# A list scheduler gets other matmul steps and a shared VectorE/GpSimd port

## The chip, the cores and the metric

The kernel runs on one core of a Trainium2 chip. The core has five engines that run their own instruction streams in order: TensorE (PE in the profile, with its weight loads as PEld), VectorE (DVE), ScalarE (ACT), GpSimd (POOL) and SyncE (SP, which here only issues DMAs). The metric is the device time of one launch in microseconds, as the median of several runs. Lower is better.

## What is computed

Two layers of a hybrid decoder on a sequence of 512 tokens with 1024 features, and a final RMS norm. Every layer has two branches that are merged by gates, an output projection and a feed-forward part:

```python
def hybrid_layer(x, c, positions, cos, sin, w_ada, b_ada, w_in, ...):
    mod = (c @ w_ada + b_ada)[:, None, :]
    sh_m, sc_m, g_m, sh_f, sc_f, g_f = jnp.split(mod, 6, axis=-1)
    h = rms_norm(x) * (1 + sc_m) + sh_m
    proj = h @ w_in
    x_lru, q_down, kv_down, k_rope, gate_a, gate_b = jnp.split(proj, IN_SPLIT_POINTS, axis=-1)
    y_a = rg_lru(causal_depthwise_conv(x_lru, conv_w, conv_b), positions, ...)
    y_b = mla(q_down, kv_down, k_rope, cos, sin, ...)
    y = jax.nn.sigmoid(gate_a) * y_a + jax.nn.sigmoid(gate_b) * y_b
    x = x + g_m * (y @ w_out)
    h = rms_norm(x) * (1 + sc_f) + sh_f
    gate, up = jnp.split(h @ w_ffn_in, 2, axis=-1)
    return x + g_f * ((jax.nn.silu(gate) * up) @ w_ffn_out)
```

`c` is one vector of 1024 numbers, so the modulation is a matrix by a vector. `rg_lru` is a recurrence over the tokens (a scan), `mla` an attention with 8 heads. All inputs are float32.

## The kernel before

Activations lie feature-major: a tile is [128 features, 512 tokens]. A product is made of three matmuls per 128x128 weight block, because both factors are split into a high and a low part in a reduced float32 type (`mm3`: high x high, high x low, low x high). Of a weight block that lands by DMA in `raw`, ScalarE makes the high part `whi` and VectorE the low part `wlo` (in the first products GpSimd makes `wlo` for the feature tiles 1 to 7). There are three buffers each of `raw`, `whi` and `wlo`, two of `graw` (the weights of the modulation), and eight PSUM banks.

The start is special. The first products (`first_products`) run by feature tile 0 to 7 into six accumulators at once, 17 matmuls per tile, each tile as soon as its scale and shift are known. Scale and shift come from columns of `w_ada` (`first_mods`): for some tiles TensorE multiplies them (`pt<-cols,wa`, plain float32, 64 columns), for the others VectorE sums them up (`wacc<-wa,cols,wacc`) and TensorE only adds over partitions (`pt<-ones,wacc`). The result lands in `mod0_0` and `mod0_1`, and ScalarE and VectorE then make the tiles `hh` and `hl` that the products take.

After that come, in layer 0 and again in layer 1: the recurrent branch (`x_lru`, `conv` with its three steps `xc`, `gates`, `decay`, `recur` with the scan `ri<-a,ri`), the attention (`make_qk`, `scores`, `transposes` with `pl<-pt,ph`, `values`), the gates, the merge, the output projection and the feed-forward products. In layer 0 VectorE also sums up the other modulation vectors in the background (`macc<-graw,cols,macc`).

What sets the order: the body does not issue instructions but records them. `order()` then plays a greedy schedule with assumed durations (`cost`), latencies and buffer counts. Whenever an engine is free in that play, it takes the ready call with the longest remaining path. The calls are issued in the order of the play, and each engine of the chip runs its own list strictly in that order, with the waits that the data needs. So a figure in `cost` decides only where an instruction stands.

There is one exception to "same calls". While TensorE is idle in the play and the first products are not through, `fill()` puts in a matmul on zeros, as many as fit the idle time, so that the clock of TensorE stays up:

```python
            if o is None or self.fill not in issued or self.fill_end in issued or now < FILL_FROM or fills[0] >= FILL_MAX:
                return
            fills[0] += 1
            busy["PE"] = True
            res.append(o)
            heapq.heappush(events, (now + clock(now, o.dur, True), next(seq), "free", "PE"))
```

A fill is 256 columns in bfloat16, and no result hangs on it; but whatever stands behind it on TensorE comes after it.

## Time and profile before

| what | value |
|---|---|
| median of 3 runs (lowest to highest) | 1367.15 us (1366.49 to 1367.56) |
| span of the profiled execution, first to last instruction | 1361.9 us |
| median less that span | 5.3 us |
| TensorE busy | 1339.6 us, 98% |
| VectorE / ScalarE / GpSimd busy | 872.4 / 623.5 / 213.2 us |
| mean granted TensorE clock | 0.995 |
| TensorE matmul records, of them fills | 6330, 57 |

The profile gives no other time of the profiled execution than its span, so the 5.3 us around it are taken from the median. In a row of the trace the first number is the start in us from the span's start and the second how long it took; "[... <-X]" is the idle time of the engine before it and what ended it. Every call goes through one helper line, so all rows read L503, and tiles have to be told by their names. The matmuls are pipelined: one of 512 columns reads 0.39 us long while the next starts 0.227 us after it, so the step from start to start counts, and the gaps that the trace calls idle are shorter than the time lost.

### The profile page before, as it was taken

How to read it: one execution, taken by the hardware profiler on the slowest of the kernel's cores; microseconds unless marked ns; L12 is line 12 of the kernel's file. 1: busy time of each engine (PE TensorE's matmuls, PEld its weight loads, DVE VectorE, ACT ScalarE, POOL GpSimd, SP SyncE). 2: the span in 40 equal slices, each digit the busy share in tenths (PEclk: the TensorE clock that was granted, in tenths of full speed). 3: DMA queues.
4: the chain of work that ended last, by engine and by line, in shares of the span. 5: the costliest groups of instructions: out<-in, count | busy, mean ns of one | idle time of the engine just before them, and what ended most of it. 6: DMA issues, size and time to landing. Idle time of an engine off the chain costs nothing.

```text
span 1361.9 us, 17108 instructions
## 1 busy us (share of the span) xinstructions
PE 1339.6 (98%) x6330; PEld 1117.8 (82%) x6330; DVE 872.4 (64%) x1478; ACT 623.5 (46%) x963; POOL 213.2 (16%) x238
## 2 busy tenths in 40 slices
PE   8999989999999999999999999999999999999997
PEld 7788878887888888888888888888888888888887
DVE  5898799788856455556869887667673333333344
ACT  5585856644432222322356767855452322232223
POOL 1613334413000000000040243413400000000000
PEclk9999989999999999999999999999999999999999
DMA  9636344334655556555635333311433323433232
GB/s 300 200 96 168 103 124 140 124 117 137 194 182 164 163 159 206 178 170 184 203 86 141 92 86 100 94 47 47 124 89 98 89 75 104 120 93 95 77 88 81
DMA packets 251297, 174.92 MB, mean 128 GB/s; under 512 B 12767, under 2 KB 235341, under 8 KB 251213
## 3 DMA queue, kind: packets, MB, share of 16 engines
q1 hardware_dynamic: 251212, 173.82, 42.3%
q8 instruction: 50, 0.82, 0.2%
q14 instruction: 35, 0.28, 0.1%
HBM read 167.50 MB, written 2.10 MB: 125 GB/s over the span
## 4 chain that ended last, share of the span: by engine, by line
PE 84%; DVE 6%; DMA 5%; issue 2%; POOL 1%; ACT 1%; SPq 1%; ACTq 0%; DVEq 0%; POOLq 0%
PE mm L503 75%; PE s L503 4%; PE o L503 3%; DMA graw<-in_w_ada_dram 2%; PE pt L503 2%; DMA wa<-in_w_ada_dram 2%; DMA raw<-in_w_in_dram 1%; DVE macc L503 1%; DVE ri L503 1%; DVE wlo L503 1%; DVE xc L503 1%; POOL w L503 1%; DVE wacc L503 1%; SPq L503 1%; DVE sc L503 0%
## 5 line engine op out<-in xcount | busy, mean ns | idle before, releaser
L503 ACT ACTIVATE whi<-raw 128x1024 fp32r<-128x1024 f32 (+2 forms) x226 | 219.7, 973 | 581.3 <-PE mm L503 371.1
L503 DVE TENSOR_TENSOR wlo<-raw,whi 128x1024 fp32r<-128x1024 f32 (+2 forms) x218 | 249.3, 1145 | 205.5 <-ACT whi L503 201.2
L503 PE MATMUL mm<-fh,wlo 128*128 128x512 f32 x672 | 261.9, 390 | 0.0
L503 PE MATMUL mm<-fh,whi 128*128 128x512 f32 x672 | 261.7, 389 | 0.0
L503 PE MATMUL mm<-fl,whi 128*128 128x512 f32 x672 | 261.6, 389 | 0.0
L503 PE MATMUL mm<-hh,whi 128*128 128x512 f32 x408 | 161.3, 396 | 0.0
L503 PE MATMUL mm<-hl,whi 128*128 128x512 f32 x408 | 160.2, 393 | 0.0
L503 PE MATMUL mm<-hh,wlo 128*128 128x512 f32 x400 | 156.3, 391 | 0.0
L503 PEld LDWEIGHTS mm<-fl,whi 128*128 128x128 f32 x672 | 126.1, 188 | 26.4 <-DVE fl L503 0.2
L503 PEld LDWEIGHTS mm<-fh,wlo 128*128 128x128 f32 x672 | 126.1, 188 | 26.4 <-DVE wlo L503 0.3
L503 PEld LDWEIGHTS mm<-fh,whi 128*128 128x128 f32 x672 | 126.2, 188 | 26.0
L503 PE MATMUL mm<-ah,whi 128*128 128x512 f32 (+1 forms) x363 | 139.7, 385 | 0.0
L503 PE MATMUL mm<-ah,wlo 128*128 128x512 f32 (+1 forms) x363 | 139.3, 384 | 0.0
L503 PE MATMUL mm<-al,whi 128*128 128x512 f32 (+1 forms) x363 | 139.0, 383 | 0.0
L503 DVE SCALAR_TENSOR_TENSOR macc<-graw,cols,macc 128x512 f32<-128x512 f32 x140 | 103.8, 777 | 24.1 <-DMA graw<-in_w_ada_dram 23.7
L503 DVE TENSOR_TENSOR sg<-sg,mm 128x512 f32<-128x512 f32 x42 | 28.9, 688 | 111.1 <-PE mm L503 111.1
L503 PEld LDWEIGHTS mm<-hl,whi 128*128 128x128 f32 x408 | 77.0, 189 | 15.5 <-DVE hl L503 0.5
L503 PEld LDWEIGHTS mm<-hh,whi 128*128 128x128 f32 x408 | 77.0, 189 | 15.1 <-DVE whi L503 0.2
L503 PEld LDWEIGHTS mm<-hh,wlo 128*128 128x128 f32 x400 | 75.4, 189 | 15.8 <-POOL wlo L503 0.3
L503 PEld LDWEIGHTS mm<-ah,wlo 128*128 128x128 f32 x363 | 68.2, 188 | 13.3
L503 PEld LDWEIGHTS mm<-al,whi 128*128 128x128 f32 x363 | 68.2, 188 | 13.1
L503 PEld LDWEIGHTS mm<-ah,whi 128*128 128x128 f32 x363 | 68.2, 188 | 13.1
(266 smaller groups left out, 2173.9 us busy)
## 6 DMA issues: line engine op xcount, KB each, us to landing
raw<-in_w_ffn_in_dram SPq DMA_DIRECT2D x88, 512.0 KB, 3.9
graw<-in_w_ada_dram SPq DMA_DIRECT2D x80, 512.0 KB, 4.8
raw<-in_w_in_dram SPq DMA_DIRECT2D x49, 512.0 KB, 4.0
raw<-in_w_ffn_out_dram SPq DMA_DIRECT2D x32, 384.0 KB, 3.5
raw<-in_w_ffn_out_dram SPq DMA_DIRECT2D x32, 320.0 KB, 3.2
wa<-in_w_ada_dram SPq DMA_DIRECT2D x32, 256.0 KB, 5.6
raw<-in_w_out_dram SPq DMA_DIRECT2D x16, 512.0 KB, 3.9
raw<-in_w_uq_dram SPq DMA_DIRECT2D x24, 128.0 KB, 3.5
```

Source lines behind the costliest of these rows:

```text
L503: o.call(*(real(v) for v in o.a), **{k: real(v) for k, v in o.k.items()})
```

## The change

Three things in the planner change. The assumed TensorE time of a float32 matmul that is not in the reduced type falls from at least 207 ns to at least 107 ns. That of a matmul in the reduced type (all the `mm3` products) rises: 512 columns from 213.5 to 223.8 ns, 128 columns from 53.4 to 106 ns; 3 ns are added to each as before. And a VectorE or GpSimd call of the kinds tensor_tensor and scalar_tensor_tensor with two wide inputs in SBUF is now `shared`: when the other engine runs such a call in the play, it waits for its end.

```diff
-                 "npred", "ready", "bytes", "live")
+                 "npred", "ready", "bytes", "live", "shared")
...
         op.dur = self.cost(op, eng, method, a, k, outs, ins)
+        op.shared = eng in ("DVE", "POOL") and method in ("tensor_tensor", "scalar_tensor_tensor") and 2 == sum(
+            isinstance(x, Ref) and x.root.tag not in BANKS and x.shape[-1] > 1 for x in ins
+        )
...
             op.live = n > 32
-            return max(207.0, n * 1.667) if lhs.dtype == F32 else max(53.0, n * 0.417)
+            if lhs.dtype == F32:
+                return max(107.0, n * 1.667)
+            return n * 0.417 if lhs.dtype == BF16 else max(106.0, n * 0.417 + 10.3)
...
+        shared = {"DVE": 0.0, "POOL": 0.0}
...
                     d = clock(now, d, o.live)
+                if o.shared:
+                    other = "POOL" if e == "DVE" else "DVE"
+                    d += max(0.0, shared[other] - now)
+                    shared[e] = now + d
```

The rest of the diff deletes comments, which moves the helper line from L503 to L513. The calls are the same ones, except that TensorE gets 198 fills in place of 57 (141 more matmuls) and ScalarE 58 table loads in place of 51. The lists of all engines differ by shifts over a few places.

The first place is TensorE's list in the first products, at feature tile 5 (`hh_42`, `hl_50`, `whi_132`, `wlo_133`); `pt_120` is the scale and shift of the tiles 6 and 7. Before:

```order
247 L503 MATMUL mm_57_365<-hl_49_587,whi_118_595 128x512
248 L503 MATMUL mm_57_365<-hh_41_556,wlo_119_607 128x512
249 L503 MATMUL o_58_369<-hh_41_556,whi_118_595 128x512
250 L503 MATMUL o_58_369<-hl_49_587,whi_118_595 128x512
251 L503 MATMUL pt_120_657<-ones_83,wacc_125_539 128x64 x2
252 L503 MATMUL mm_53_345<-hh_42_565,whi_132_611 128x512
253 L503 MATMUL mm_53_345<-hl_50_628,whi_132_611 128x512
254 L503 MATMUL mm_53_345<-hh_42_565,wlo_133_630 128x512
255 L503 MATMUL pt_120_657<-ones_83,wacc_130_544 128x64 x2
```

Now, where the pair of rows 464 and 465 is the last of 41 fills that stand there one behind the other:

```order
464 L513 LDWEIGHTS fill_w_77
465 L513 MATMUL fill_4_87<-fill_x_75,fill_w_77 128x256
466 L513 MATMUL mm_53_384<-hl_50_756,whi_132_639 128x512
467 L513 MATMUL mm_53_384<-hh_42_646,wlo_133_668 128x512
468 L513 MATMUL mm_54_389<-hl_50_756,whi_132_639 128x512
469 L513 MATMUL mm_54_389<-hh_42_646,wlo_133_668 128x512
470 L513 MATMUL s_55_391<-hl_50_756,whi_132_639 128x512
471 L513 MATMUL s_55_391<-hh_42_646,wlo_133_668 128x512
472 L513 MATMUL s_56_396<-hl_50_756,whi_132_639 128x512
473 L513 MATMUL pt_120_786<-ones_83,wacc_125_594 128x64 x2
474 L513 MATMUL s_56_396<-hh_42_646,wlo_133_668 128x512
475 L513 MATMUL mm_57_402<-hl_50_756,whi_132_639 128x512
```

The six `hh` x `whi` matmuls of tile 5 have gone ahead of the fills, and the scale and shift of the tiles 6 and 7 (`pt_120`) have gone behind them and behind seven more products. Another 22 fills follow at row 479 and 15 more six matmuls later.

The second place is VectorE's list in layer 0, at the convolution step `xc_395`, which reads the PSUM bank `mm_394`, and at the attention tiles `pl_411` and `pl_405`. `ri_212<-a_383`, `ri_255<-a_364` and `ri_260<-a_389` are scans. Before:

```order
263 L503 TENSOR_TENSOR xcl_382_1886<-xc_380_1828,xch_381_1878 128x512
264 L503 TENSOR_SCALAR sg_354_1847<-sg_354_1847 128x512
265 L503 SCALAR_TENSOR_TENSOR ri_212_1082<-a_383_1806,ri_212_1082 128x512
266 L503 SCALAR_TENSOR_TENSOR xc_395_1889<-mm_394_1823,cols2_638,xc_395_1889 128x511
267 L503 SCALAR_TENSOR_TENSOR ri_255_1228<-a_364_1656,ri_255_1228 128x512
268 L503 SCALAR_TENSOR_TENSOR xc_395_1889<-mm_394_1823,cols2_638,xc_395_1889 128x510
269 L503 TENSOR_TENSOR wlo_476_1917<-raw_474_1864,whi_475_1901 128x1024
270 L503 SCALAR_TENSOR_TENSOR xc_395_1889<-mm_394_1823,cols2_638,xc_395_1889 128x509
271 L503 SCALAR_TENSOR_TENSOR ri_260_1246<-a_389_1842,ri_260_1246 128x512
272 L503 TENSOR_TENSOR yt_385_1777<-yt_385_1777,ri_194_1077 128x512
273 L503 TENSOR_TENSOR pl_411_1962<-pt_409_1931,ph_410_1955 128x512
```

Now:

```order
255 L513 TENSOR_TENSOR xcl_382_2045<-xc_380_1979,xch_381_2028 128x512
256 L513 SCALAR_TENSOR_TENSOR xc_395_2021<-mm_394_1971,cols2_779,xc_395_2021 128x511
257 L513 TENSOR_TENSOR wlo_476_2066<-raw_474_1994,whi_475_2033 128x1024
258 L513 SCALAR_TENSOR_TENSOR xc_395_2021<-mm_394_1971,cols2_779,xc_395_2021 128x510
259 L513 SCALAR_TENSOR_TENSOR ri_212_1213<-a_383_1914,ri_212_1213 128x512
260 L513 SCALAR_TENSOR_TENSOR xc_395_2021<-mm_394_1971,cols2_779,xc_395_2021 128x509
261 L513 TENSOR_TENSOR pl_411_2101<-pt_409_2068,ph_410_2089 128x512
262 L513 TENSOR_TENSOR pl_405_2108<-pt_403_2056,ph_404_2094 128x512
263 L513 TENSOR_TENSOR pl_408_2114<-pt_406_2063,ph_407_2099 128x256
264 L513 TENSOR_TENSOR xcl_397_2120<-xc_395_2021,xch_396_2104 128x512
265 L513 TENSOR_TENSOR ql_421_2124<-mm_419_2087,qh_420_2111 128x512
266 L513 SCALAR_TENSOR_TENSOR ri_255_1370<-a_364_1797,ri_255_1370 128x512
```

Two of the three scans and the step `yt_385` have gone behind the three `pl` steps; one scan is left ahead of the last `xc_395`.

## Rows read from the trace of the kernel before

**Rows 1.** The page's head: the span, TensorE's busy time, the clock in 40 slices and the chain of work that ended last, by engine.

```profile
span 1361.9 us, 17108 instructions
...
PE 1339.6 (98%) x6330; PEld 1117.8 (82%) x6330; DVE 872.4 (64%) x1478; ACT 623.5 (46%) x963; POOL 213.2 (16%) x238
...
PEclk9999989999999999999999999999999999999999
...
PE 84%; DVE 6%; DMA 5%; issue 2%; POOL 1%; ACT 1%; SPq 1%; ACTq 0%; DVEq 0%; POOLq 0%
```

**Rows 2.** Stretches of the span. Columns: from and to in us, length; busy time and instructions of PE, PEld, DVE, ACT and POOL; granted TensorE clock; share of the DMA engines; GB/s.

```profile
45.01:52.88 7.87, 5.73 (x33) 4.47 (x32) 7.87 (x10) 2.19 (x5) 6.91 (x6) 1.00 0.44 120
52.88:59.39 6.51, 6.51 (x25) 5.46 (x26) 2.77 (x7) 5.22 (x8) 4.97 (x7) 0.74 0.73 198
...
140.00:170.00 30.00, 29.03 (x147) 24.57 (x147) 23.94 (x56) 24.94 (x45) 10.66 (x13) 1.00 0.32 99
...
178.00:184.00 6.00, 3.00 (x13) 2.17 (x12) 6.00 (x7) 2.77 (x7) 3.15 (x2) 1.00 0.08 18
184.00:192.00 8.00, 7.47 (x20) 5.17 (x19) 8.00 (x14) 5.21 (x7) 2.92 (x2) 0.58 0.76 249
192.00:340.00 148.00, 146.39 (x747) 124.64 (x745) 125.95 (x250) 80.05 (x144) 46.12 (x52) 1.00 0.42 129
...
760.00:830.00 70.00, 69.08 (x355) 58.72 (x354) 56.73 (x123) 53.25 (x92) 27.17 (x26) 1.00 0.34 91
...
1340.00:1361.90 21.90, 14.86 (x108) 13.77 (x106) 8.14 (x27) 6.89 (x12) 0.00 (x0) 0.91 0.26 97
```

**Rows 3.** What TensorE waited for from 0 to 67.2 us, that is up to the end of the first products: us in total, times, longest.

```profile
PE pt L503 <- DVE cols L503: 2.1, 1, 2.1
PE pt L503 <- DVE mod L503: 2.1, 2, 1.8
PE fill L503 <- DVE fill_w L503: 1.3, 1, 1.3
PE mm L503 <- DMA ident<-in_consts_dram: 1.0, 1, 1.0
PE pt L503 <- DVE wacc L503: 0.4, 1, 0.4
PE pt L503 <- DMA wa<-in_w_ada_dram: 0.4, 1, 0.4
```

**Rows 4.** TensorE in order of time in the first products: fills, small float32 matmuls, and what follows them.

```profile
11.96 0.93 PE L503 MATMUL fill<-fill_x,fill_w 128*128 128x256 bf16 x7
12.72 1.90 PE L503 MATMUL pt<-cols,wa 128*128 128x64 f32 x16
14.46 0.82 PE L503 MATMUL fill<-fill_x,fill_w 128*128 128x256 bf16 x6
...
31.84 0.66 PE L503 MATMUL pt<-ones,wacc 128*128 128x64 f32 x4 [1.79 <-DVE mod L503]
...
32.62 0.39 PE L503 MATMUL s<-hh,whi 128*128 128x512 f32 x1
32.85 0.40 PE L503 MATMUL s<-hl,whi 128*128 128x512 f32 x1
...
45.01 1.70 PE L503 MATMUL fill<-fill_x,fill_w 128*128 128x256 bf16 x14
46.47 0.48 PE L503 MATMUL mm<-hh,whi 128*128 128x512 f32 x1
...
52.88 0.66 PE L503 MATMUL pt<-ones,wacc 128*128 128x64 f32 x4 [2.15 <-DVE cols L503]
...
55.30 0.63 PE L503 MATMUL mm<-hl,whi 128*128 128x512 f32 x1
55.73 0.63 PE L503 MATMUL mm<-hh,wlo 128*128 128x512 f32 x1
```

**Rows 5.** The chain that ended last, in the feed-forward part of layer 0: 219 matmuls of 512 columns that follow each other without a wait.

```profile
387.66 49.76 PE mm L503 x219
```

**Rows 6.** TensorE in order of time around 180 us.

```profile
179.65 0.39 PE L503 MATMUL mm<-cnh,pwl 128*128 128x512 f32 x1
183.04 0.47 PE L503 MATMUL mm<-cnh,pwh 128*128 128x512 f32 x1 [3.00 <-DVE xc L503]
...
185.26 0.79 PE L503 MATMUL pt<-cnh,rwh 128*128 128x512 f32 x1 [0.53 <-DVE pl L503]
```

**Rows 7.** VectorE in order of time in the same stretch (the second place of the section above).

```profile
175.61 2.30 DVE L503 TENSOR_TENSOR_SCAN ri<-a,ri 128x512 f32<-128x512 f32 x1
...
178.48 1.61 DVE L503 TENSOR_TENSOR_SCAN ri<-a,ri 128x512 f32<-128x512 f32 x1
...
182.16 0.73 DVE L503 SCALAR_TENSOR_TENSOR xc<-mm,cols,xc 128x509 f32<-128x509 f32 x1
182.81 1.21 DVE L503 TENSOR_TENSOR_SCAN ri<-a,ri 128x512 f32<-128x512 f32 x1
183.94 0.66 DVE L503 TENSOR_TENSOR yt<-yt,ri 128x512 f32<-128x512 f32 x1
184.53 1.28 DVE L503 TENSOR_TENSOR pl<-pt,ph 128x512 fp32r<-128x512 f32 x2
```

**Rows 8.** The table loads of ScalarE, as one group: busy time, mean ns of one, idle time before.

```profile
L503 ACT ACT_TABLE_LOAD x51 | 65.4, 1283 | 1.8 <-PEq L1538 0.7 <-DVE mx L503 0.3
```

## The prediction

> **What bounds the kernel now.** I read the head of the page first: TensorE is busy for 1339.6 of 1361.9 us, the chain that ended last is 84% TensorE, and the clock falls below full speed in few slices [rows 1]. VectorE, next, has 64%. So the time is the TensorE list itself plus what TensorE stands still, and an order can change only two things: the idle 1361.9 - 1339.6 = 22.3 us and what the clock costs. Where these lie I read next, by stretches [rows 2]: 3.00 us in 178 to 184, 0.53 in 184 to 192, 1.61 over the 148 us after that, 0.97 in 140 to 170, 0.92 in 760 to 830, 7.04 in the tail; and 7.2 us of waits up to 67.2 us [rows 3]. The clock costs 6.51 x 0.26 = 1.7 us at 52.88, 8.00 x 0.42 = 3.4 us at 184 and 21.9 x 0.09 = 2.0 us in the tail [rows 2]. All of it together, 29.4 us, is the most that any order could win, and the tail is the same in both lists. Last I read the durations of what is added [rows 4], the step of a long product [rows 5], and the second place of the change on TensorE and VectorE [rows 6, 7].
>
> **Part 1: the fills.** This is the one part that adds work to the bounding engine: 141 more matmuls on zeros, all ahead of the end of the first products. In the trace seven fills take from 11.96 to 12.72, 0.109 us each, and fourteen take from 45.01 to 46.47, 0.104 us each [rows 4]. 141 x 0.104 = 14.7 and 141 x 0.109 = 15.4; I take 15.0 us.
>
> Why does the planner see so much idle time? A small float32 matmul of 64 columns is two records in the trace: 16 records from 12.72 to 14.46 are 8 instructions at 0.218 us [rows 4]. The planner's old figure (207 + 3 ns) fits that; the new one (107 + 3) is the time of one record, half the instruction. There are 51 of them (40 with `cols`, 11 with `ones`), so the play has 51 x 0.108 = 5.5 us of TensorE time that the chip doesn't have, room for 53 fills. The other 88 come from a play that now makes VectorE and GpSimd wait for each other.
>
> What can these 15 us lie beside? Of the waits up to 67.2 us, 1.3 us stand ahead of the first fill and 1.0 for the first constants; the other 2.1 + 2.1 + 0.4 + 0.4 = 5.0 us can be filled [rows 3]. There are six such gaps, and at each a matmul reads 0.39 us long where its step is 49.76 / 219 = 0.227 us [rows 5, 6]; the 0.16 us of difference are lost time that the trace doesn't call idle: 6 x 0.16 = 1.0 us. Last, the stretch 52.88 to 59.39, which follows the wait of 2.15 us, was granted 0.74 [rows 2, 4]: one matmul to the next took 55.73 - 55.30 = 0.43 us there [rows 4], about twice 0.227, so that engine ran at 1.2 in place of 2.4 GHz for part of it. With 41 fills ahead of that place the wait and the dip should both go: 1.7 us. So 15.0 - 5.0 - 1.0 - 1.7 = **+7.3 us** at the end of the first products, some 74.5 us in place of 67.2. Bounds of this term: +15.0 if nothing is absorbed, and +4 if VectorE's own shifts (the `pt_120` and `hl_50` steps) let the last tiles come closer together; 7.3 is nearer to what the rows give.
>
> The Trainium skill, page "TensorE: Matmul & The Clock Gate", section "Wait — 56ns, not 53.3ns?", says that warm back-to-back matmuls start N / 2.4 GHz plus about 2.5 ns apart, which by that page is about 29 ns for 64 columns. By it the 51 small matmuls would cost an estimated 1.5 us rather than 51 x 0.218 = 11.1, the surplus of 7.3 would turn into a spare of about 2, and the fills would be hidden. The trace disagrees here (0.218 us for the float32 instruction of 64 columns [rows 4]), and the measurement decides.
>
> **Part 2: the steps of the long products.** 223.8 + 3 = 226.8 ns in the planner against 227.2 in the trace [rows 5]; the old 216.5 was 5% short. This changes no instruction, only the play's clock against the other engines, so by itself it costs nothing; it bears on part 4.
>
> **Part 3: the order around 180 us.** TensorE waits 3.00 us for the last step of `xc` [rows 6]. Three steps of `xc` read that bank on VectorE, with scans between them, the last one at 182.16 [rows 7]; VectorE is busy for 6.00 of 6.00 us in 178 to 184 [rows 2]. A scan there takes 2.30, 1.61 or 1.21 us [rows 7]. In the new list one scan fewer is left ahead of the last step; with the 1.61 us one gone the wait falls from 3.00 to about 1.4. The wait of 0.53 us for `pl` [rows 6] goes, as two scans and `yt` (1.61 or 1.21 each, and 0.66 [rows 7]) are no longer ahead of `pl`. That is 1.6 + 0.5, with rounding up for the drains **-2.2 us**; bounds 0 and -3.8 (all of 3.53 and two drains). Then the clock: 184 to 192 was granted 0.58 [rows 2], right behind that wait. Dips stand behind the waits of 2.15 and 3.00 us, none behind the one of 1.79 at 31.84, where the matmuls that follow have their usual step (32.85 - 32.62 = 0.23 us) [rows 4, 6]. A rest of 1.4 us is shorter than that, so I let the dip go: **-3.4 us**, bounds 0 and -3.4.
>
> **Part 4: everything else.** The lists of the five engines shift by a few places through both layers. Where TensorE has the longer stretches of small waits (140 to 170 and 760 to 830) these come to 0.97 + 0.92 = 1.9 us [rows 2], now chosen well or by luck. A new order can lose these or add as much: bounds -1.9, and above the seven added table loads of ScalarE, 7 x 1.283 = 9.0 us [rows 8], if TensorE waited for every one. ScalarE is busy for 46% [rows 1], and the 65.4 us of loads it has now end in hardly any wait of TensorE, so I cost them at nothing by themselves. For new waits I take **+1.9 us**, as much as there are: the old list was worked out with steps 5% short, which errs towards work being ready early, and the new one without that reserve.
>
> Sum: 15.0 - 5.0 - 1.0 - 1.7 - 2.2 - 3.4 + 1.9 = **+3.6 us** on 1361.9, so 1365.5 us. The median of the runs is 5.3 us above that span; I carry that along: **1370.7 us**, 0.26% above 1367.15. 0.2%, about what can be told from no change here, is 2.7 us.
>
> **The rivals.**
>
> First, the whole surplus is won back by about 192 us, and the time stays: 7.3 - 3.5 (both waits) - 0.3 (drains) - 3.4 (clock) = +0.1, with +1.9 behind it 2.0 us: 1367 to 1369. For it speaks that VectorE, not TensorE, sets the pace at 178 to 184 (6.00 of 6.00 against 3.00 [rows 2]): a TensorE that comes 7 us later finds its data ready. Against it: the three scans wait for ScalarE's tiles, which come of TensorE's own gate products and shift with it.
>
> Second, faster. The mechanism is the shared port in the play: a VectorE step that stands beside a GpSimd step is known to be late, so the play puts the one that TensorE needs ahead everywhere, and the waits go not only at 180 us but in 140 to 170, 192 to 340 and 760 to 830 too (0.97 + 1.61 + 0.92 = 3.5 us [rows 2]). With 7.3 - 3.8 - 3.4 - 3.5 = -3.4 the time is near 1364. The floor is what is left when all goes but the start's first 2.3 us and the tail's 7.0 + 2.0: 15.0 - (29.4 - 11.3) = -3.1, and some 18 drains at 0.16 less, -6.0, or 1361. It decides from the point where TensorE's waits behind 67 us fall under about 1.5 us in all. For it: GpSimd works in all these stretches. Against it: TensorE was already at 98%, and what the order wins must first pay for the fills.
>
> Third, slower by much: nothing is won back at 180 us because the `xc` steps themselves start later, and a few of the added table loads stand in TensorE's way. 7.3 + 0 + 1.9 = +9.2, or 1376; with half of the 9.0 us of loads +13.8, or 1381. For it: 51 small matmuls priced at half; against it: ScalarE's spare time.
>
> Fourth, the change doesn't do what it says: the play comes no nearer to the chip, because one price was set right and one wrong. The fills then still cost their 7.3 us, the waits at 180 us and the dip stay, and gains and losses elsewhere cancel: 1374.5. It lies within the forecast's side.
>
> **How the numbers follow.** The forecast with its own spread (dip gone or not, waits of 0 to 1.9: +2.7 to +8) has 0.38; the first rival 0.30; faster 0.20; the third 0.08; the fourth 0.04. Slower by over 0.2%: 0.38 + 0.08 + 0.04 = 0.50; within 0.2%: 0.30; faster: 0.20. The likeliest case alone reaches from 1370 to 1375. The range takes in most of the faster case and of the third: 1361 to 1379.
>
> **What would show it.** Fills: a group of 198 instead of 57 at 0.104 to 0.109 us, and the first products ending near 74.5 us; under 70 would say that something else than TensorE paced the start. The dip at 52.88 to 59.39 gone: clock 1.00 behind the fills. At about 187 us: TensorE's wait for `xc` at 1.4 us or less, none for `pl`, and a clock near 1.00 in the 8 us that follow; a clock of 0.6 there makes part 3 wrong. ScalarE: 58 table loads and no wait of TensorE for them. Steps of the long products: 0.227 as before, since nothing in them changes. The forecast is wrong if TensorE's idle time behind the first products falls below 8 us with the tail's 7.04 in it (then faster), or if a new wait of over 3 us stands anywhere behind 192 us.

## The result, and the profile after

The changed kernel takes 1385.83 us (median of 4 runs, 1384.68 to 1387.37) where the kernel before took 1367.36 (1366.49 to 1367.81). The ratio is 1.0141, 95% interval 1.0127 to 1.0156: 19 us slower. The direction was forecast, the size was not: 1370.7 was predicted, 1379 was the upper end.

The head of the page of the changed kernel answers to [rows 1]:

```profile
span 1382.8 us, 17402 instructions
...
PE 1354.8 (98%) x6471; PEld 1130.7 (82%) x6471; DVE 875.3 (63%) x1478; ACT 634.2 (46%) x970; POOL 203.2 (15%) x238
```

TensorE's busy time grew by 15.2 us and its idle time from 22.3 to 28.0. That reads as if the fills were the loss. They are not: busy time includes matmuls at half clock, and a gain in one place hides a loss in another. To see where time was lost I put the two traces side by side at the same point of the work: the start of the n-th TensorE record, fills not counted (6273 records in either trace). The difference of the two starts is how late the changed kernel is there.

| place | before, us | after, us | late by, us | new in this stretch |
|---|---|---|---|---|
| last part of the first products (record 260) | 63.5 | 70.8 | +7.3 | +7.3 |
| ahead of the first scores (480) | 110.8 | 119.2 | +8.4 | +1.1 |
| behind them (510) | 116.3 | 132.0 | +15.8 | +7.4 |
| ahead of the last `xc` (810) | 178.7 | 193.0 | +14.2 | -1.5 |
| behind it (840) | 192.5 | 200.7 | +8.2 | -6.1 |
| output projection (1540) | 329.4 | 343.7 | +14.3 | +6.1 |
| behind the statistics (1600) | 343.5 | 361.1 | +17.6 | +3.3 |
| last record | 1355.1 | 1376.0 | +21.0 | +3.4 |

The last row says 21.0 us, the medians 18.5. In every later run the traced execution's time lies 1.7 to 1.9 us above its span (1384.68 against 1382.8 here); by that the traced execution of before took some 1363.7 us (an estimate), 3.5 under its median. Executions of one list differ as well. Three later runs have before's list up to 175 us, and they start record 260 from 1.2 us earlier to 3.5 later than the trace of before, and record 480 from 3.2 to 5.7 later; three others have the changed list up to record 480 and stand there 6.2 to 8.2 us late (8.4 in the table). So a step of several us within a short stretch can be trusted, a lateness as such only to some 5 us.

The waits of TensorE, the longest first (us in total, times, longest), answer to [rows 3, 6]:

```profile
PE s L513 <- ACT qh L513: 4.3, 1, 4.3
PE o L513 <- DVE sacc L513: 4.1, 3, 3.2
PE o L513 <- DVE mred L513: 2.7, 2, 1.3
PE pt L513 <- DVE rwl L513: 2.1, 1, 2.1
```

The old leaders, `xc` with 3.0 and `cols` with 2.1, have gone, and four new ones stand in their place. In order of time, with what stands around two of them:

```profile
74.39 0.28 PE L513 MATMUL fill<-fill_x,fill_w 128*128 128x256 bf16 x1
...
77.45 1.05 PE L513 MATMUL o<-ones,sacc 128*128 128x1 f32 x8 [0.50 <-DVE sacc L513]
...
119.62 0.39 PE L513 MATMUL s<-xch,lwl 128*128 128x512 f32 x1
124.27 1.44 PE L513 MATMUL s<-kh,qh 128*128 128x512 f32 x4 [4.26 <-ACT qh L513]
...
194.88 0.50 PE L513 MATMUL mm<-cnh,pwh 128*128 128x512 f32 x1 [0.61 <-DVE xc L513]
...
203.61 0.50 PE L513 MATMUL pt<-cnh,rwl 128*128 128x512 f32 x1 [2.06 <-DVE rwl L513]
...
354.60 1.05 PE L513 MATMUL o<-ones,sacc 128*128 128x1 f32 x8 [3.21 <-DVE sacc L513]
```

The last fill, which closes the first products, stands at 74.39 where it stood at 67.11. The end of the first products and the stretches behind these waits, with the columns of [rows 2] (the granted clock is the third number from the end):

```profile
45.00:59.40 14.40, 14.40 (x99) 11.62 (x98) 13.73 (x19) 5.65 (x9) 9.61 (x8) 1.00 0.47 138
60.00:74.20 14.20, 14.20 (x87) 11.80 (x86) 9.13 (x16) 9.43 (x15) 10.23 (x21) 1.00 0.38 105
76.00:84.00 8.00, 7.50 (x35) 6.08 (x34) 5.42 (x17) 5.80 (x10) 0.69 (x1) 0.79 0.35 81
124.27:131.10 6.83, 6.83 (x24) 6.06 (x25) 4.22 (x10) 5.69 (x6) 2.38 (x2) 0.54 1.02 313
190.00:198.00 8.00, 7.39 (x38) 5.89 (x38) 8.00 (x12) 6.16 (x9) 1.34 (x2) 1.00 0.40 131
198.00:206.00 8.00, 5.94 (x27) 4.49 (x26) 8.00 (x9) 2.81 (x6) 3.39 (x2) 1.00 0.00 0
354.50:359.30 4.80, 4.70 (x18) 3.78 (x19) 1.83 (x8) 1.32 (x2) 0.00 (x0) 0.64 0.37 109
```

Behind the wait of 4.26 us TensorE ran near 1.2 GHz for 6.8 us (0.54), which costs 6.83 x 0.46 = 3.1 us more. At 190 us, the same work that had 0.58 before, the clock is now full.

Why does `qh` come late? ScalarE has the answer. Its list has the split `whi` of a weight block ahead of `kh` and `qh` now, and SyncE, which issues the block's DMA, shows the other half. First ScalarE, then SyncE, both in order of time:

```profile
114.61 2.73 ACT L513 ACTIVATE ri<-s,cols 128x512 f32<-128x512 f32 x4
122.19 1.06 ACT L513 ACTIVATE whi<-raw 128x1024 fp32r<-128x1024 f32 x1 [4.84 <-DMA raw<-in_w_in_dram]
123.15 0.58 ACT L513 ACTIVATE kh<-mm 128x512 fp32r<-128x512 f32 x1
123.62 0.59 ACT L513 ACTIVATE qh<-mm 128x512 fp32r<-128x512 f32 x1
```

```profile
111.76 1.84 SPq L513 DMA_DIRECT2D stk<-oh  x3
113.65 1.21 SPq L513 DMA_DIRECT2D stk<-ol  x2
114.92 0.58 SPq L513 DMA_DIRECT2D stk<-oh  x1
115.55 1.22 SPq L513 DMA_DIRECT2D stk<-ol  x2
116.81 0.59 SPq L513 DMA_DIRECT2D stk<-oh  x1
117.50 0.53 SPq L513 DMA_DIRECT2D raw<-in_w_in_dram  x1
```

ScalarE stands idle for 4.84 us: the split waits for a block whose DMA was issued at 117.50, behind nine small copies, and the two steps that TensorE needs are queued behind the split. ScalarE before, at the same work:

```profile
109.63 0.60 ACT L503 ACTIVATE qh<-mm 128x512 fp32r<-128x512 f32 x1 [0.46 <-PE mm L503]
110.31 0.60 ACT L503 ACTIVATE kh<-mm 128x512 fp32r<-128x512 f32 x1
112.72 1.06 ACT L503 ACTIVATE whi<-raw 128x1024 fp32r<-128x1024 f32 x1 [1.81 <-DMA raw<-in_w_in_dram]
```

There `qh` and `kh` stand ahead of the split, and it waits for its DMA with nothing behind it that TensorE had to wait for. The copies are not the difference: before, the block's DMA was issued at 107.79, behind ten of them.

The wait at 354.60 has another cause. VectorE (first fence) and GpSimd (second), in order of time:

```profile
348.03 5.91 DVE L513 TENSOR_TENSOR wlo<-raw,whi 128x1024 fp32r<-128x1024 f32 x1 [0.16 <-ACT whi L513]
353.86 0.68 DVE L513 TENSOR_TENSOR sacc<-sacc,sq 128x512 f32<-128x512 f32 x1
```

```profile
348.12 2.54 POOL L513 TENSOR_TENSOR wsa<-wsa,wsb 128x512 f32<-128x512 f32 x2
350.62 2.23 POOL L513 TENSOR_TENSOR wsa<-wsa 128x256 f32<-128x256 f32 x4
```

A weight split that takes 1.23 us elsewhere takes 5.91 here. It ends at 353.94, 1.1 us behind the end of GpSimd's six sums (352.85), as if it had stood still while they ran.

### The profile page after: what moved, and what is told of

Same layout as the page of the kernel before. It is cut to its first block, busy times and chain, and to the rows that moved or that the text cites. A ratio compares the mean times of both kernels' runs of the same rounds, so it can differ in the third digit from the quotient of the medians.

```text
span 1382.8 us, 17402 instructions
## 1 busy us (share of the span) xinstructions
PE 1354.8 (98%) x6471; PEld 1130.7 (82%) x6471; DVE 875.3 (63%) x1478; ACT 634.2 (46%) x970; POOL 203.2 (15%) x238
## 4 chain that ended last, share of the span: by engine, by line
PE 85%; DVE 7%; ACT 3%; DMA 2%; issue 2%; POOL 1%; SPq 0%; ACTq 0%; DVEq 0%
PE mm L513 74%; PE s L513 5%; PE o L513 3%; PE pt L513 2%; PE fill L513 1%; DMA graw<-in_w_ada_dram 1%; DVE wlo L513 1%; DVE macc L513 1%; DVE xc L513 1%; DVE ri L513 1%; POOL w L513 1%; DMA xtok<-in_x_dram 1%; ACT whi L513 1%; ACT L513 0%; DVE xcl L513 0%
## 5 line engine op out<-in xcount | busy, mean ns | idle before, releaser
L513 ACT ACTIVATE whi<-raw 128x1024 fp32r<-128x1024 f32 (+2 forms) x226 | 219.9, 973 | 587.1 <-PE mm L513 373.0
L513 DVE TENSOR_TENSOR wlo<-raw,whi 128x1024 fp32r<-128x1024 f32 (+2 forms) x218 | 252.2, 1159 | 217.1 <-ACT whi L513 215.5
L513 PE MATMUL mm<-fl,whi 128*128 128x512 f32 x672 | 261.8, 390 | 0.0
L513 PE MATMUL mm<-fh,whi 128*128 128x512 f32 x672 | 261.4, 389 | 0.0
L513 PE MATMUL mm<-fh,wlo 128*128 128x512 f32 x672 | 261.3, 389 | 0.0
L513 PE MATMUL mm<-hh,whi 128*128 128x512 f32 x408 | 161.0, 397 | 0.4 <-DVE ql L513 0.4
L513 PE MATMUL mm<-hl,whi 128*128 128x512 f32 x408 | 160.4, 393 | 0.0
L513 PE MATMUL mm<-hh,wlo 128*128 128x512 f32 x400 | 156.8, 392 | 0.0
L513 PEld LDWEIGHTS mm<-fh,wlo 128*128 128x128 f32 x672 | 126.1, 188 | 26.2
L513 PEld LDWEIGHTS mm<-fl,whi 128*128 128x128 f32 x672 | 126.2, 188 | 26.1
L513 PEld LDWEIGHTS mm<-fh,whi 128*128 128x128 f32 x672 | 126.1, 188 | 26.1
L513 PE MATMUL mm<-ah,wlo 128*128 128x512 f32 (+1 forms) x363 | 139.6, 384 | 0.0
L513 PE MATMUL mm<-al,whi 128*128 128x512 f32 (+1 forms) x363 | 139.3, 384 | 0.0
L513 PE MATMUL mm<-ah,whi 128*128 128x512 f32 (+1 forms) x363 | 139.1, 383 | 0.0
L513 DVE SCALAR_TENSOR_TENSOR macc<-graw,cols,macc 128x512 f32<-128x512 f32 x140 | 104.6, 786 | 20.0 <-DMA graw<-in_w_ada_dram 19.8
L513 DVE TENSOR_TENSOR sg<-sg,mm 128x512 f32<-128x512 f32 x42 | 28.9, 688 | 105.0 <-PE mm L513 105.0
L513 PEld LDWEIGHTS mm<-hh,whi 128*128 128x128 f32 x408 | 77.0, 189 | 15.7 <-DVE ql L513 0.9
L513 PEld LDWEIGHTS mm<-hl,whi 128*128 128x128 f32 x408 | 77.2, 189 | 14.9
L513 PEld LDWEIGHTS mm<-hh,wlo 128*128 128x128 f32 x400 | 75.7, 189 | 15.7
L513 PEld LDWEIGHTS mm<-al,whi 128*128 128x128 f32 x363 | 68.2, 188 | 13.4
L513 PEld LDWEIGHTS mm<-ah,whi 128*128 128x128 f32 x363 | 68.2, 188 | 13.1
L513 PEld LDWEIGHTS mm<-ah,wlo 128*128 128x128 f32 x363 | 68.2, 188 | 13.0
```

The source lines that it names most:

```text
L513: o.call(*(real(v) for v in o.a), **{k: real(v) for k, v in o.k.items()})
```

## Experiments

Times are ratios to runs of the kernel before on the same chip, with their interval; in us, times 1367. "Late" is always the difference of the table above, against the same trace of before, with the spread given there. Three theories stood at first: P, the shared port makes the bad order; F, the added fills cost it; O, any new order finds its own new waits.

**Each of the three changes alone, and the two prices without the port.**

```diff
-            return max(207.0, n * 1.667) if lhs.dtype == F32 else max(53.0, n * 0.417)
+            return max(107.0, n * 1.667) if lhs.dtype == F32 else max(53.0, n * 0.417)   # small price alone
+            return max(207.0, n * 1.667) if lhs.dtype == F32 else max(106.0, n * 0.417 + 10.3)   # long price alone
```

(shortened: in every run the fills, which are bfloat16, keep their 0.417 ns a column)

> The kernel before with the shared port alone (old prices of both kinds of matmul); 155 fills. Theory P (the port rule makes the bad order): nearly all of the 19 us, +13 to +20 us, with waits of TensorE behind 70 us as in the changed kernel. Theory F (it is the fills): 98 fills more are 10.2 us, of which some 7.7 find room, so +2 to +3 us. Theory O (any new order finds its own new waits, whichever price makes it): +5 to +15 us, and the place at 119 us need not be among them.

> The kernel before with the price of 107 ns for the small float32 matmuls alone; 100 fills. P: no change within 2 us. F: 43 fills are 4.5 us and find room, no change within 2 us. O: +5 to +15 us by new waits behind 70 us.

> The kernel before with the longer steps of the reduced-type matmuls alone (223.8 and 106 ns); 51 fills, 6 fewer than before. P: no change within 2 us. F: no change, or a gain of up to 0.6 us. O: +5 to +15 us by new waits behind 70 us, and the first products end at 67 us as before.

> The changed kernel without the shared port: both new prices; 93 fills. P: back to the time before within 3 us. F: 36 fills more find room, so within 2 us of before. O: still +5 to +15 us.

| kernel | fills | ratio (interval) | us |
|---|---|---|---|
| port alone | 155 | 1.0067 (1.0044 to 1.0089) | +9 |
| small price alone | 100 | 0.9998 (0.9982 to 1.0014) | 0 |
| long price alone | 51 | 1.0150 (1.0116 to 1.0185) | +20.5 |
| both prices, no port | 93 | 1.0123 (1.0093 to 1.0153) | +17 |
| all three (the change) | 198 | 1.0141 (1.0127 to 1.0156) | +19 |

The long price alone costs as much as all three changes, with six fills fewer than before. F falls, P falls. The parts don't add up: the port costs 9 us by itself, and on top of both prices 2 or 3, within the intervals. O's range holds the port, but the small price moves nothing and the long one lies above it; the place at 119 us is lost with the long price (7.4 us there), and only 1.7 us of it with the port alone. The long price of 512 columns is also the true one: 226.8 ns against a measured step of 227.2 [rows 5]. The wrong one, 107 ns for an instruction that takes 218, costs nothing. One thing was not taken apart: the long price also doubles the price of 128 columns (53.4 to 106 ns), and which of the two makes the order slow was not run.

**Fewer fills in the changed order.**

```diff
-            res.append(o)
+            if fills[0] * 57 // 198 != (fills[0] - 1) * 57 // 198:
+                res.append(o)
```

> The changed kernel's own order, but of each 198 fills of the play only 57 are issued, spread evenly; they write zeros that nothing reads. By the prediction's first part the first products end some 6 to 7 us earlier, near 68 us. If the surplus is then kept: 1379 us. If what comes later eats it up (VectorE sets the pace at 180 us): less than 3 us are won, 1383 us or more.

1.0110 (1.0092 to 1.0128). The first products end at 71.86 in place of 74.39, with a wait of 4.0 us for the first constants in that execution (1.5 in the changed kernel's, for other constants); without that difference of 2.5 us they would end at about 69.4, one or two us later than expected. At the end 1 to 4 us of it are left (1.4 by the medians, 4 by the ratios), and the profiled executions end within 1.1 us of each other. So the fills are at most a few of the 19 us; of the two outcomes expected, the one in which what comes later eats the gain up is what came (1384.41 us, 1383 or more expected).

**The split behind `q`, and the sums off GpSimd.** In the list that the planner returns, two instructions are moved; in the second run the six `wsa` sums also go to VectorE, behind the statistics.

```diff
+        for e, name, behind in (("ACT", "whi_309", "qh_263"), ("DVE", "wlo_310", "ql_264")):
+            o = next(o for o in res if o.eng == e and out(o) == name)
+            res.remove(o)
+            res.insert(1 + max(i for i, q in enumerate(res) if q.eng == e and out(q) == behind), o)
...
+        for o in mine:   # the tensor_tensor calls on wsa_782 and wsa_784
+            res.remove(o)
+            o.eng, o.call = "DVE", tt
+        res[at:at] = mine
```

> The changed kernel with one place put back by hand: on ScalarE the split whi_309 of a weight block goes behind qh_263 and kh_266, and on VectorE wlo_310 behind ql_264. If that place is the cause of the loss at 120 us: the wait of 4.3 us for qh and the half clock behind it go, and TensorE is 6 to 7.5 us earlier at 130 us. At the end 4 to 7 us are left of it if nothing later takes it back, under 2 us if the waits around 190 us grow by as much.

> As the run before, and the six sums of wsa in the middle of layer 0, which GpSimd does while VectorE makes a weight split that takes 5.91 us in place of 1.23, now stand on VectorE behind the statistics. If VectorE was held up there by GpSimd: that split takes 1.2 us again, the wait of 3.2 us for sacc goes, and the time is 3 to 5 us under that of the run before. If the two have nothing to do with each other: the same time within 1 us, or slower by the 2.9 us of added VectorE work.

The first move: 1.0122 (1.0106 to 1.0138), little or nothing won. TensorE loses 4.9 us at the first scores in place of 7.4, for the split still stood in front of somebody:

```profile
119.68 0.83 PE L518 MATMUL s<-kh,qh 128*128 128x512 f32 x4
123.59 0.63 PE L518 MATMUL mm<-hh,whi 128*128 128x512 f32 x1 [3.07 <-ACT ri L518]
```

`ri` empties the PSUM bank that the next product takes, and it too stands behind the split on ScalarE.

The second: 1.0065 (1.0043 to 1.0087), 7.4 us under the first by the medians, more than the 3 to 5 expected. On VectorE, in order of time, the same split is short again:

```profile
343.15 1.23 DVE L526 TENSOR_TENSOR wlo<-raw,whi 128x1024 fp32r<-128x1024 f32 x1 [0.16 <-ACT whi L526]
344.29 0.69 DVE L526 TENSOR_TENSOR sacc<-sacc,sq 128x512 f32<-128x512 f32 x1
```

From the output projection (record 1480) to the feed-forward part (2000) the run loses nothing against before (8.3 us late, then 8.2), where the run with the first move alone goes from 11.5 to 19.7. So GpSimd's sums held VectorE up, and this one collision is worth 7 to 8 us between these two runs (in the changed kernel itself the same stretch loses 4.1).

**The split one place further back.** The same list with the sums on VectorE, and `whi_309` behind `ri_276` as well.

> The changed kernel with the sums on VectorE as in the earlier run, and the split whi_309 one place further back on ScalarE, behind ri_276, which frees the bank that TensorE waited 3.07 us for when only qh and kh had gone ahead. If the place at 120 us is only this split that waits for its DMA: TensorE loses less than 2 us there (7.4 in the changed kernel, 4.9 with the first move), and the time is 2 to 5 us under the run with both moves, that is 1374 to 1377 us. If another wait takes its place again: no gain.

1.0068 (1.0048 to 1.0089): no better than the run before it, as far as the intervals of 0.2% tell. The place itself is mended (1.0 us is lost at the first scores in place of 7.4; the longest wait there is 0.6 us for `kl`), but between there and the end the gain is lost again in the traces, 2.9 us of it in layer 1, where the two runs have the same list (8.2 to 10.6 us late in the one, 6.0 to 11.3 in the other). That part can be spread: the traced execution of the run with both moves took 1374.29 us, 4.2 under its median. What a place gives back is not what the kernel gets.

**Other true prices.** In the changed kernel, small float32 matmuls, scans, DMA issues and table loads were priced by the trace.

```diff
-                return max(107.0, n * 1.667)
+                return max(215.0, n * 1.667)
...
+            if method == "tensor_tensor_scan":
+                return 1143.0
...
-DMA_ISSUE = 470.0
+DMA_ISSUE = 600.0
...
-TABLE_LOAD = 2000.0
+TABLE_LOAD = 1283.0
```

> The changed kernel with more prices set to what the traces show: small float32 matmuls 215 ns, scans on VectorE 1143 in place of 601 ns, a DMA issue 600 in place of 470, a table load 1283 in place of 2000; the long steps and the shared port as changed. Theory C (the longer step hurts because the other engines' prices are too low beside it): the loss falls to under 6 us. Theory D (any new list brings its own waits): still +8 to +20 us over before.

1.0067 (1.0046 to 1.0089), +9 us: half of the loss goes, but not under 6, as C had it, and TensorE still waits 4.1 us for `kh`. D's range holds it at its lower end.

**A 5% shorter step, a 0.1% change either way, and half the change.** If any new order were a bad draw, a change of 0.1% should do it too, since it carries no belief about the chip. It moves fewer rows than the change, though: in the lists 106 and 144 of TensorE's 6171 calls without the fills stand at another place, 581 in the changed one.

```diff
-            return max(207.0, n * 1.667) if lhs.dtype == F32 else max(53.0, n * 0.417)
+            return max(207.0, n * 1.667) if lhs.dtype == F32 else max(53.0, n * 0.397)   # or 0.4166, 0.4174, 0.427
```

> The kernel before (old prices, no shared port) with the step of the reduced-type matmuls made 5% shorter still: 203 in place of 213.5 ns for 512 columns; 64 fills. Theory M (a step that is too short is a reserve: the play then wants everything else early): not slower than before by more than 3 us, perhaps faster by 2. Theory D (this list was a lucky draw, and any change of the step gives another list with its own waits): slower by 5 to 20 us, as the longer step was (+20.5 us).

> The kernel before with the step of the reduced-type matmuls 0.1% shorter (0.4166 in place of 0.417 ns for a column). No belief on the chip changes by this. Theory D (each list is a draw, and the one before is a good one): another list, and the time moves by 3 us or more, most likely slower. Theory L (it is the length of the step that counts, by its 5%): within 2 us of before.

> The same with the step 0.1% longer (0.4174 ns). Theory D: moves by 3 us or more, most likely slower, and not by the same places as the shorter one. Theory L: within 2 us of before.

> The kernel before with the step 2.4% longer, half way to the changed kernel's (0.427 ns for a column, 218.6 ns for 512). Theory L: about half of what the long step alone cost, +8 to +13 us. Theory D: any value from 0 to +20 us, not tied to the length.

| price for 512 columns, ns | ratio (interval) | us |
|---|---|---|
| 203.3 (-4.8%) | 1.0041 (1.0026 to 1.0056) | +6 |
| 213.3 (-0.1%) | 0.9998 (0.9984 to 1.0012) | 0 |
| 213.7 (+0.1%) | 0.9986 (0.9973 to 0.9998) | -2 |
| 218.6 (+2.4%) | 1.0056 (1.0042 to 1.0071) | +8 |
| 223.8 (+4.8%; 128 columns doubled) | 1.0150 (1.0116 to 1.0185) | +20.5 |

D falls in its strong form: small shuffles cost nothing. Both of these lists keep the order at 119 and at 180 us, so they say little on larger ones; the small price, which moves 253 of TensorE's calls, costs nothing either. M (a short step is a reserve, and more of it does no harm) falls too, since a shorter step also loses. L's 8 to 13 us for half the change are met at their lower edge. The loss grows with the distance from the old step. That it grows faster on the long side is not shown, since the last row alone has the doubled price of 128 columns in it.

**What the longer step is too long against.**

```diff
-        op.dur = self.cost(op, eng, method, a, k, outs, ins)
+        op.dur = self.cost(op, eng, method, a, k, outs, ins) * (1.048 if eng in ("DVE", "ACT", "POOL") else 1.0)
...
-DMA_LAT = 2400.0
+DMA_LAT = 4400.0
```

(the first two lines are the one run, the last two the other; both with the long price alone)

> The kernel before with the long step alone, as in the third run (+20 us), and every price of VectorE, ScalarE and GpSimd 4.8% higher, so that their ratio to the step is that of the kernel before; DMA landings, latencies and table loads are left. The split whi_309 still stands ahead of qh_263 and kh_266. Theory L1 (the step hurts by its ratio to the other engines' prices): within 4 us of before. Theory L2 (it hurts by its ratio to the time at which DMAs land in the play): still +10 us or more, and the loss at 115 us stays.

> The kernel before with the long step alone, and DMAs that land 2.0 us later in the play (4.4 in place of 2.4 us behind their bytes); all other prices as before. The split whi_309 now stands behind qh_263 and kh_266. Theory L2: the loss of 7 us at 115 us goes, and the time falls from +20 to +12 us or less. Theory L1: no change, +15 us or more.

Other engines longer: 1.0072 (1.0052 to 1.0093), +10. DMAs that land later: 1.0055 (1.0039 to 1.0072), +7.5. What TensorE waits for from 105 to 135 us, the first with the other engines longer, the second with later DMAs:

```profile
PE s L513 <- ACT qh L513: 2.7, 1, 2.7
```

```profile
PE s L513 <- DVE kl L513: 1.6, 1, 1.6
```

L1 wanted the first within 4 us of before, and falls as a whole cause, though half of the loss goes. L2's two figures are met, the first at its edge (+10 us or more; +9.8 measured), but the loss at the first scores, which it wanted to stay, is 2.9 us there in place of 7.4. With later DMAs it is 2.1 us.

Was it the DMA that the split waits for? By the order of the lists it looks so: where the split stands ahead of both `qh` and `kh` (the changed kernel, fewer fills, the long price alone, both prices, half the change, other true prices, other engines longer) TensorE waits 4.3, 4.2, 2.7, 2.0, 2.3, 4.1 and 2.7 us for one of them; where it stands behind both (before, small price alone, the shorter step and the two of 0.1%, the moved split, later DMAs, VectorE's order) it waits for neither. With the port alone it stands between the two, and TensorE waits 1.4 us for `kh`. But the wait has two causes. In the changed kernel, with fewer fills, both prices and other engines longer, ScalarE stands idle in front of the split, for the DMA (4.84, 4.79, 2.58 and 3.27 us). With the long price alone it does not:

```profile
110.81 1.04 ACT L513 ACTIVATE whi<-raw 128x1024 fp32r<-128x1024 f32 x1
...
118.78 0.63 ACT L513 ACTIVATE a<-ri 128x512 f32<-128x512 f32 x1 [2.83 <-DVE ri L513]
119.31 0.58 ACT L513 ACTIVATE kh<-mm 128x512 fp32r<-128x512 f32 x1
119.79 0.59 ACT L513 ACTIVATE qh<-mm 128x512 fp32r<-128x512 f32 x1
```

The split is through long before, and `kh` and `qh` stand behind a step that waits 2.83 us for VectorE's `ri`. Half the change and other true prices show the same with 2.69 us each, for `kh` alone. On VectorE that `ri` stands behind `wlo`, the low part of the same block (1.21 us at 116.87); with later DMAs `wlo` has gone behind `kl`, `qh` stands ahead of the step that waits, and the wait is 0.83 us. So later DMAs in the play put weight splits further back, on VectorE too, but they did not free `qh` from a DMA here.

Nor is the longer landing the truer price. A block of 512 KB lands in the play 512 KB / 360 GB/s + 2.4 = 3.9 us behind its issue when no other transfer is ahead of it, 5.9 with the later landing. The page of the changed kernel has (KB each, median us to landing):

```profile
raw<-in_w_in_dram SPq DMA_DIRECT2D x49, 512.0 KB, 4.2
```

**VectorE's order at 180 us in the kernel before.** Three runs. In the first two runs the scan `ri_212` stands behind GpSimd's product of `ri_212` with its gate, so that this product takes the values from before the scan; the instructions are the same ones.

> The kernel before with two scans of VectorE put behind the steps of xc_395 (ri_212) and behind ql_421 (ri_255), as the changed list has it, and nothing else. If the third part of the prediction is right by itself and not only because TensorE came later: the wait of 3.0 us at 180 us shrinks to under 1 us, the half clock behind it goes, and the time is 4 to 6.5 us under before. If it only worked because TensorE was 14 us late there: within 2 us of before.

> As the run before, and the six sums of wsa in the middle of layer 0 on VectorE behind the statistics in place of GpSimd. In the kernel before these stood beside the small steps of the statistics, which took 0.58, 1.20 and 0.65 us in place of 0.16 each, and TensorE waited 1.46 us. So 1 to 2 us under the run before; if VectorE's 2.9 us of added work is in the way instead, 1 to 3 us over it.

0.9989 (0.9974 to 1.0003) and 0.9987 (0.9972 to 1.0001): the 4 to 6.5 us did not come, nor the 1 to 2 us more for the sums.

The third run has the order of the changed kernel, with the scan ahead of the product:

```diff
+            ("ri_212", "tensor_tensor_scan", lambda: steps()[1]),     # behind the second step of xc_395
+            ("ri_255", "tensor_tensor_scan", lambda: last("ql_421")),
+            ("yt_385", "tensor_tensor", lambda: last("pl_405")),
```

> The kernel before with three steps of VectorE put as the changed list has them: the scan ri_212 behind the second step of xc_395, the scan ri_255 behind ql_421, the step yt_385 behind pl_405. If the third part of the prediction holds for VectorE's order alone: TensorE's wait at 180 us falls from 3.0 us to under 1, the clock of 1.2 GHz behind it goes, and the time is 3 to 6 us under before. If the changed kernel lost nothing there only because TensorE came 14 us late: at most 2 us are won in that place, and the time is within 2 us of before.

0.9996 (0.9984 to 1.0007). TensorE around this place, in order of time, and the stretch behind it:

```profile
186.87 0.47 PE L519 MATMUL mm<-cnh,pwh 128*128 128x512 f32 x1 [1.05 <-DVE xc L519]
...
188.91 0.50 PE L519 MATMUL pt<-cnh,rwh 128*128 128x512 f32 x1 [0.65 <-DVE pl L519]
...
190.56 0.65 PE L519 MATMUL pt<-cnh,rwl 128*128 128x512 f32 x1 [0.93 <-DVE rwl L519]
```

```profile
186.80:194.80 8.00, 6.36 (x19) 4.49 (x20) 8.00 (x13) 5.79 (x8) 2.61 (x3) 0.79 0.77 238
```

The one wait of 3.00 us became three, 2.6 us together, and the clock still falls behind them (0.79). The place gives 2.0 us, not 6, and the kernel nothing that can be measured. VectorE is busy for 8.00 of 8.00 us: its work was shuffled, not shortened.

## Why the prediction was wrong

**The fills (part 1) were right in size at their place.** +7.3 us at the end of the first products was forecast, and +7.3 came (7.0 by the means of the four executions of either list); 198 fills, as read from the list. That they agree to the tenth is luck: executions of one list lie up to 4.7 us apart at this place, and the sum has a slip ([rows 3] has five gaps that can be filled, not six). The wait of 2.15 us there and the half clock behind it went, as argued (1.00 from 45 to 59.4 and from 60 to 74.2 us). By the first scores the means are only 4.6 us apart. That some fills come of the wrong small price was right (43 with it alone where 53 were reckoned, 98 with the port), but beside the point: the small price alone costs nothing at the end.

**The steps (part 2) were costed at nothing by themselves, "only the play's clock against the other engines".** That price, with that of the short matmuls in it, makes the 20 us when it is changed alone. I saw the mechanism ("without that reserve") and gave it no size of its own.

**The place at 180 us (part 3) came out at -6.1 us where -5.6 was forecast, but not for good, and less than half for the reason given.** The wait for `xc` fell to 0.61 (1.4 forecast), that for `pl` went, the clock is full. But 2.4 us of the gain are lost right behind it, at the wait of 2.06 us for `rwl`, and VectorE's order alone, in the kernel before, gives 2.0. That TensorE came late to a place that VectorE paces, the first rival's argument, doesn't explain the rest: every run with the changed kernel's list, and the one with other true prices, wins 5.8 to 6.2 us there, whether TensorE comes 7.2 or 14.2 us late, and with the long price alone it comes 11.3 late and wins nothing (12.0 behind it). What else in the changed lists wins there is open.

**"New waits: +1.9 us" (part 4) is the step that failed.** The table gives what it stood for: everything but the first products and the place at 180 us, 21.0 - 7.3 + 6.1 = 19.8 us (some 17 by the medians). Of this TensorE loses 7.4 at the split that waits for its DMA in front of `qh`, with the half clock behind it; 3.3 at the collision of GpSimd's sums with a weight split; the other 9.1 at smaller places. Only the collision is shown to reach the end, with 7 us by the medians between two runs; mending the place at `qh` won nothing that could be measured. The wait of 3.21 us behind it is the sign that I had named: a new wait of over 3 us behind 192 us. I had sized the term by the waits that the old list has in two quiet stretches, which says how good that list is, not how good another one will be. The upper bound (seven table loads, 9.0 us) was of the wrong kind: 58 loads came, as read, and none of TensorE's waits names one.

**The rivals.** The third (slower by much) had the sign and a price of 9 to 14 us, but by other places than those that lost. The fourth was right that one price was set right and one wrong, but it is the right one that cost the time, and the waits at 180 us did not stay.

**What stays open.** Why the long price makes such an order is not shown. Putting DMAs later in the play takes back 13 of the 20.5 us, longer prices of the other engines 10; both together were not run, nor the price of 512 columns without that of 128. There is a rival that the runs leave standing: the old list is a good one, and any list well away from it costs 6 to 10 us (the port +9, the shorter step +6, half the change +8, other true prices +9, other engines longer +10, later DMAs +7.5). Then only the rest of the 20.5 us belongs to the long price. Whether the script of steps had been chosen with the old prices was not tried.

## What to carry to other kernels

One price in a list scheduler, made true by itself, can make the order worse, and one made less true can win much of that back: here 4.8% on the long products (with twice the price for the short ones) cost 20.5 us, and a DMA landing that the play puts 1.7 us later than the trace's median took back 13. So judge a price by the order that it makes, and change prices that meet in one decision together. Look first at what stands at the head of an engine's queue when its input is late, as `whi` before `qh` in the changed kernel. And a forecast for a new order has to price the waits it may bring by what such an order can do, not by the waits that the old one happens to have.

## What the runs showed of the hardware

A VectorE and a GpSimd instruction with two inputs in SBUF held each other up. In the changed kernel the split's record starts at 348.03, GpSimd's sums' at 348.12, and the split stood until all six sums were through; in the run with the first move it is the same again (5.91 us), and with fewer fills (5.90). With both prices and no port the sums' record starts first (344.06 against 344.18), and the split takes 5.67. With the long price alone the split comes 2.3 us behind the first sum, takes 1.34, and the four small sums then take 4.13 us in place of 2.23. The Trainium skill, page "SBUF — State Buffer", section "SBUF: two separate sides", says that whichever starts first gets the shared pair for the whole instruction and the other blocks. The full block agrees (5.91 against 1.23 us). Who starts first can't be told from records 0.1 us apart, and in four of these five runs the block lasted over six instructions, not one.

The clock did not follow the length of the last wait as I had read it. A wait of 2.15 us had half clock behind it before, one of 2.06 at 203.61 had none (the stretch 198 to 206 reads 1.00 with TensorE busy for 5.94 of 8 us). From 76 to 84 us it reads 0.79 behind a wait of 0.5 us, where sixteen matmuls of one column follow; before, the same sixteen behind a wait of 1.00 us had none (1.00 from 70 to 78). In the last run on VectorE's order three waits of 1.05, 0.65 and 0.93 us close together had 0.79 behind them. So small waits can cost clock too: 8 us at 0.79 are 1.7 us, as much as the dip behind the wait of 2.15 us.
